# Routing of a PEER layer: picked places compared, multiplied and summed on VectorE, place numbers shifted and masked once per head

## Chip, core and metric

The kernel runs on one core of a Trainium2 chip. The metric is the device time of one execution in microseconds (us). Engines are called as in the profile: PE (TensorE), DVE (VectorE), ACT (ScalarE), POOL (GpSimd), SP (SyncE, which issues most DMAs).

## What is computed

Two layers of a decoder trunk over 512 tokens of width 1024. Each layer: a modulated norm and one wide projection; an S5 state-space branch; a causal differential attention; gates, an output projection and a residual; then a PEER stage over 128 x 128 single-neuron experts. The change lies in PEER's routing, per token and for 8 heads:

```python
v1, i1 = lax.top_k(s1, 16)            # s1, s2: scores against 128 keys each
v2, i2 = lax.top_k(s2, 16)
cand = (v1[..., :, None] + v2[..., None, :]).reshape(..., 256)
sc, ci = lax.top_k(cand, 16)
e1 = jnp.take_along_axis(i1, ci // 16, axis=-1)
e2 = jnp.take_along_axis(i2, ci % 16, axis=-1)
expert = e1 * 128 + e2
g = jax.nn.softmax(sc, axis=-1)
```

The picked experts' rows of two tables are then used with weights from g and a GELU.

## The kernel before

Tokens lie in four tiles of 128. Tiles 1 to 3 are served densely: all 128 chunks of 128 experts are scored by TensorE, and per token weights, zero for experts that were not picked, are built from the routing by `gates`. Tile 0 is served sparsely: its picked rows are gathered.

`front` holds everything of a layer up to the gates. At its end two streams are interleaved: `routed((1, 2, 3))`, which is `route` for three tiles and then `gates`, and `tail`, which already scores 36 of the 128 chunks (`experts`, `products`: a chunk's table is loaded, cast on ACT (L130), its rest subtracted (L132, here on POOL), and 24 matmuls of three lines, L135 to L137, follow on PE). The program's order is only a wish: a scheduler decides each engine's own order when the kernel is built, and each engine then works through its list in that order and waits where it must.

`route(tiles, ...)` runs m = len(tiles) steps per head, 24 in all for tiles 1 to 3, and 8 for tile 0, whose `route` runs in `sparse` beside the dense stage. A step (hp, j) has

- `ask`: query projection of the next head on PE (L833), copied to SBUF by ACT (pqT, L835);
- `halves`: two score matmuls (L840), then `top16` twice on DVE straight from PSUM (MAX8, MATCH_REPLACE8, FIND_INDEX8), the 16 places cast to floats on ACT (i16f, L846), and the 256 candidate sums on POOL (cand, L848);
- `pairs`, one step later: `top16` over the candidates, place numbers ci; ci >> 4 and ci & 15 on DVE (ij, L857 and L858), cast on ACT (ijf, L860);
- `picked`, two steps later: DVE compares ijf with the numbers 0 to 15 (oh, L866: two halves x 16 places x 16 numbers = 512 elements per partition), POOL multiplies by i16f (L868);
- three steps later DVE sums the products into e12 (L886).

For tiles 1 to 3 the numbers 0 to 15 are read from `at`, a copy in PSUM; for tile 0 from `iota128` in SBUF. After the last step the softmax over csv is made (L894 to L900), and `gates` begins for tile 1: transpositions of e12 and csv on PE (L912, L913), eg on ACT, then 16 times a comparison on DVE (L920), products on POOL (L922) and ACT (L925), and outer products on PE (L938).

`layer_consts` (L141) loads small constants of a layer; lt (L153) holds the four lambda vectors, in a tile of its own in pool sm. `sgt()` (L124) hands out one of three buffers sg of 128 x 512, which the S5 tables, the expert products and others use in turn. Pool sm has three buffers per name where nothing else is said, pool rt one.

Of the kernel before, what the change touches and what calls it, by code (L numbers as in the profile page):

```python
# [11 lines left out]
F32 = mybir.dt.float32  # L12
# [3 lines left out]
U32 = mybir.dt.uint32  # L16
AF = mybir.ActivationFunctionType
ALU = mybir.AluOpType
AX = mybir.AxisListType
# [8 lines left out]
TOPK = 16  # L28
# [32 lines left out]
def trunk(ctx, tc, x, c, ada_w, ada_b, n1, n2, w_in, log_dt, a_re, a_im, b_re, b_im, c_re, c_im, dsk,  # L61
          glu_w, qn, kn, lam, subln, up_w, w_out, wq, pk, u_tab, v_tab, u_t, out):
    nc = tc.nc
    V, S, G, T = nc.vector, nc.scalar, nc.gpsimd, nc.tensor
# [10 lines left out]
    sm = ctx.enter_context(tc.tile_pool(name="sm", bufs=3))  # L75
# [48 lines left out]
    def sgt():  # L124
        return sgp.tile([128, 512], F32, name="sg")
# [15 lines left out]
    def layer_consts(l):  # L141
        dc = keep.tile([128, 4], F32, name=f"dc{l}")
        nc.sync.dma_start(dc, dsk[l])
        dcols.append(dc)
        col = keep.tile([128, 3], F32, name=f"col{l}")
        nc.sync.dma_start(col[:, 0:1], qn[l])
        nc.sync.dma_start(col[:, 1:2], kn[l])
        nc.sync.dma_start(col[:, 2:3], subln[l])
        linit = 0.8 - 0.6 * math.exp(-0.3 * l)
        V.tensor_scalar(col[:, 0:1], col[:, 0:1], 0.125, None, op0=ALU.mult)  # L150
        V.tensor_scalar(col[:, 2:3], col[:, 2:3], 1.0 - linit, None, op0=ALU.mult)
        cols.append(col)
        lt = sm.tile([128, 4, 64], F32, name="lt", bufs=1)  # L153
        nc.sync.dma_start(lt, lam[l:l + 1].to_broadcast([128, 4, 64]))
        V.tensor_tensor(lt[:, 0:2], lt[:, 0:2], lt[:, 2:4], op=ALU.mult)
        l2 = sm.tile([128, 2], F32, name="l2")
        V.reduce_sum(l2, lt[:, 0:2], axis=AX.X)
        S.activation(l2, l2, AF.Exp)
        nl = keep.tile([128, 1], F32, name=f"nlam{l}")
        V.tensor_tensor(nl, l2[:, 1:2], l2[:, 0:1], op=ALU.subtract)  # L160
        V.tensor_scalar(nl, nl, linit, None, op0=ALU.subtract)
        lams.append(nl)
        k2 = keep.tile([128, 2, 128], F32, name=f"pk{l}")
        nc.sync.dma_start(k2, pk[l])
        pks.append(k2)
# [286 lines left out]
    def tok(i):  # L452
        return slice(128 * i, 128 * i + 128)
# [32 lines left out]
    def front(l, xsrc, mcol, raw, last, big, rstack, fp, mmp, bup, trp, atp, spec, tail):  # L486
# [326 lines left out]
        def top16(src, n, vals, ids):  # L813
            tmp = rt.tile([128, 256], F32, name="tmp")
            V.max(vals[:, 0:8], src)
            V.match_replace(tmp[:, :n], vals[:, 0:8], src, NEG)  # L816
            V.max(vals[:, 8:16], tmp[:, :n])
            V.max_index(ids[:, 0:8], vals[:, 0:8], src)
            V.max_index(ids[:, 8:16], vals[:, 8:16], tmp[:, :n])

        def route(tiles, pqt, pst, io):

            m, wide = len(tiles), [128, 2, TOPK, TOPK]
            steps = [(hp, j) for hp in range(PH) for j in range(m)]
            query, st = {}, {}

            def ask(hp, s):
                if s == 0:
                    query[hp] = rt.tile([128, 2, ND], F32, name="pqT", bufs=2), load_w(wq[l], 256 * hp, D, nw=256)
                pqT, w = query[hp]  # L830
                pq = pqt()[:, :128 * m]
                for k in range(8):
                    T.matmul(pq.rearrange("p (t n) -> p t n", n=128), w[k][:, 128 * s:128 * s + 128], hts[tiles][:, :, k],  # L833
                             start=(k == 0), stop=(k == 7))
                S.copy(pqT[:, s, :128 * m], pq)  # L835

            def halves(hp, j):
                pss = pst()
                for s in range(2):
                    T.matmul(pss[:, 128 * s:128 * s + 128], query[hp][0][:, s, tok(j)], pks[l][:, s], start=True, stop=True)  # L840
                v16 = sm.tile([128, 2, TOPK], F32, name="v16")
                i16 = sm.tile([128, 2, TOPK], U32, name="i16")
                for s in range(2):
                    top16(pss[:, 128 * s:128 * s + 128], 128, v16[:, s], i16[:, s])
                i16f = sm.tile([128, 2, TOPK], F32, name="i16f")
                S.copy(i16f, i16)  # L846
                cand = rt.tile([128, TOPK, TOPK], F32, name="cand", bufs=2)
                G.tensor_tensor(cand, v16[:, 0].unsqueeze(2).to_broadcast([128, TOPK, TOPK]),  # L848
                                v16[:, 1].unsqueeze(1).to_broadcast([128, TOPK, TOPK]), op=ALU.add)
                st[hp, j] = i16f, cand  # L850

            def pairs(hp, j):
                i16f, cand = st[hp, j]
                ci = sm.tile([128, TOPK], U32, name="ci")
                top16(cand.rearrange("p a b -> p (a b)"), 256, csv[tiles[j]][:, hp], ci)
                ij = sm.tile([128, 2, TOPK], U32, name="ij")
                V.tensor_single_scalar(ij[:, 0], ci, 4, op=ALU.logical_shift_right)  # L857
                V.tensor_single_scalar(ij[:, 1], ci, 15, op=ALU.bitwise_and)  # L858
                ijf = sm.tile([128, 2, TOPK], F32, name="ijf")
                S.copy(ijf, ij)  # L860
                st[hp, j] = i16f, ijf

            def picked(hp, j):
                i16f, ijf = st[hp, j]
                oh = rt.tile([128, 2, TOPK, TOPK], F32, name="oh", bufs=1)
                V.tensor_tensor(oh, ijf.unsqueeze(3).to_broadcast(wide),  # L866
                                io[:, 0:TOPK].unsqueeze(1).unsqueeze(1).to_broadcast(wide), op=ALU.is_equal)
                G.tensor_tensor(oh, oh, i16f.unsqueeze(2).to_broadcast(wide), op=ALU.mult)  # L868
                st[hp, j] = oh

            for i in tiles:
                e12[i] = rt.tile([128, 2, PH, TOPK], F32, name="e12", bufs=3)
            ask(0, 0)
            ask(0, 1)
            for n in range(len(steps) + 3):
                if n < len(steps):
                    hp, j = steps[n]
                    halves(hp, j)
                    for s in range(2):
                        if hp + 1 < PH and j == max(m - 2 + s, 0):  # L880
                            ask(hp + 1, s)
                if 0 <= n - 1 < len(steps):
                    pairs(*steps[n - 1])
                if n >= 3:
                    hp, j = steps[n - 3]
                    V.reduce_sum(e12[tiles[j]][:, :, hp], st.pop((hp, j)), axis=AX.X)  # L886
                if 0 <= n - 2 < len(steps):
                    picked(*steps[n - 2])
                if n < len(steps):
                    yield 5  # L890
            for i in tiles:
# [54 lines left out]
        mg, hts, e12, xts = {}, {}, {}, {}  # L946
        csv = {i: keep.tile([128, PH, TOPK], F32, name=f"csv{i}" + ("" if i in DENSE else f"_{l}")) for i in range(4)}
# [29 lines left out]
        with phase(f"l{l}", [("lp", 1)], []) as (tp,):  # L977
            rt = rstack.enter_context(tc.tile_pool(name=f"r{l}", bufs=1))
# [323 lines left out]
```

## Time and profile before

| what | us |
|---|---|
| median of 3 runs | 3679.18 (3678.8 to 3679.29) |
| the profiled execution, its own time | 3686.12 |
| its span, first to last instruction | 3684.4 |
| busy: PE, DVE, ACT, POOL | 3503.5, 2635.5, 1386.9, 1304.4 |
| routing of tiles 1 to 3 | 508 to 691 in layer 0, 2330 to 2514 in layer 1 |
| gates | 716 to 873 and 2540 to 2697 |

The span is 1.7 us shorter than the execution's time. Busy times are unions of the records of an engine; matmuls are pipelined and their ends are modelled, so that a busy PE need not be PE at its peak. A wait is the idle time of an engine before an instruction, put down to what ended it.

### The profile page before, as it was taken

How to read it: one execution, taken by the hardware profiler on the slowest of the kernel's cores; microseconds unless marked ns; L12 is line 12 of the kernel's file. 1: busy time of each engine (PE TensorE's matmuls, PEld its weight loads, DVE VectorE, ACT ScalarE, POOL GpSimd, SP SyncE). 2: the span in 40 equal slices, each digit the busy share in tenths (PEclk: the TensorE clock that was granted, in tenths of full speed). 3: DMA queues.
4: the chain of work that ended last, by engine and by line, in shares of the span. 5: the costliest groups of instructions: out<-in, count | busy, mean ns of one | idle time of the engine just before them, and what ended most of it. 6: DMA issues, size and time to landing. Idle time of an engine off the chain costs nothing.

```text
span 3684.4 us, 50752 instructions
## 1 busy us (share of the span) xinstructions
PE 3503.5 (95%) x18546; PEld 2928.1 (79%) x18546; DVE 2635.5 (72%) x5033; ACT 1386.9 (38%) x2403; POOL 1304.4 (35%) x931
## 2 busy tenths in 40 slices
PE   8998999899999999999999989998999999999999
PEld 6764677798888888888888647677988888888888
DVE  5855267867678887788977453687666777778887
ACT  3353232475333333333342532325633333333332
POOL 1101134552025554444411001445511544544442
PEclk8998999999999999999999989999999999999999
DMA  7634243478679998998855242435775888999986
GB/s 236 205 115 152 88 149 101 147 220 274 208 277 315 339 327 317 328 339 315 308 198 170 87 152 86 155 115 165 219 252 169 302 327 318 326 329 334 334 313 221
DMA packets 404358, 859.97 MB, mean 233 GB/s; under 512 B 37470, under 2 KB 206430, under 8 KB 400012
## 3 DMA queue, kind: packets, MB, share of 16 engines
q1 hardware_dynamic: 317488, 578.68, 46.0%
q0 software_dynamic: 74304, 270.57, 20.6%
q10 hardware_dynamic: 12316, 7.47, 0.8%
q8 instruction: 146, 2.39, 0.3%
q14 instruction: 104, 0.85, 0.1%
HBM read 769.94 MB, written 86.68 MB: 233 GB/s over the span
## 4 chain that ended last, share of the span: by engine, by line
PE 65%; DVE 15%; DMA 8%; POOL 4%; ACT 4%; issue 2%; SPq 0%; POOLq 0%; DVEq 0%; ACTq 0%
PE acc L135 8%; PE acc L136 8%; PE acc L137 8%; PE sc L135 7%; PE sc L137 7%; PE sc L136 7%; DMA big<-wd 6%; PE mm L547 4%; PE bu L938 3%; PE mm L137 3%; PE mm L135 2%; PE mm L136 2%; DVE wh L132 2%; POOL oh L868 1%; DVE tmp L816 1%
## 5 line engine op out<-in xcount | busy, mean ns | idle before, releaser
L130 ACT CAST wh<-wt 128x1024 fp32r<-128x1024 f32 x592 | 620.7, 1050 | 1008.9 <-PE sc L135 477.1
L132 DVE TENSOR_TENSOR wh<-wt,wh 128x1024 fp32r<-128x1024 f32 x520 | 635.6, 1226 | 254.0 <-ACT wh L130 247.9
L135 PE MATMUL sc<-hh,wh 128*128 128x384 f32 (+1 forms) x2112 | 730.3, 346 | 11.3 <-DVE wh L132 5.6
L137 PE MATMUL sc<-hh,wh 128*128 128x384 f32 (+1 forms) x2112 | 714.2, 338 | 0.0
L136 PE MATMUL sc<-hl,wh 128*128 128x384 f32 (+1 forms) x2112 | 712.4, 338 | 0.3 <-DVE hl L474 0.3
L135 PE MATMUL acc<-wh,gl 128*128 128x512 f32 x1536 | 618.3, 403 | 41.0 <-DVE gl L1042 40.5
L136 PE MATMUL acc<-wh,gh 128*128 128x512 f32 x1536 | 610.5, 397 | 0.5 <-DVE wh L132 0.5
L137 PE MATMUL acc<-wh,gh 128*128 128x512 f32 x1536 | 610.8, 398 | 0.0
L1095 POOL DMA_INDIRECT gt<-in_u_tab_dram,idx x256 | 402.7, 1573 | 390.9 <-DVE junk L1103 330.5
L1095 POOL DMA_INDIRECT gt<-in_v_tab_dram,idx x256 | 343.3, 1341 | 457.3 <-DVE acc L1107 393.6
L135 PEld LDWEIGHTS sc<-hh,wh 128*128 128x128 f32 x2112 | 404.1, 192 | 25.6 <-DVE wh L132 7.1
L136 PEld LDWEIGHTS sc<-hl,wh 128*128 128x128 f32 x2112 | 403.9, 191 | 12.6 <-DVE hl L474 0.6
L137 PEld LDWEIGHTS sc<-hh,wh 128*128 128x128 f32 x2112 | 403.3, 191 | 0.3
L135 PEld LDWEIGHTS acc<-wh,gl 128*128 128x128 f32 x1536 | 290.6, 189 | 111.7 <-DVE gl L1042 52.2
L137 PEld LDWEIGHTS acc<-wh,gh 128*128 128x128 f32 x1536 | 290.6, 189 | 70.9
L136 PEld LDWEIGHTS acc<-wh,gh 128*128 128x128 f32 x1536 | 291.1, 190 | 60.8 <-ACT wh L130 0.9
L1107 DVE SCALAR_TENSOR_TENSOR acc<-gt,act,acc 128x1024 f32<-128x1024 f32 x254 | 326.8, 1287 | 2.3
L1103 DVE SCALAR_TENSOR_TENSOR junk<-gt,h 128x1024 bf16<-128x1024 f32 x256 | 312.0, 1219 | 2.2 <-DMA gt<-in_u_tab_dram,idx 0.3
L920 DVE TENSOR_TENSOR big<-eg,at 128x2048 f32<-128x2048 f32 x96 | 218.9, 2286 | 101.0 <-PE bu L938 44.9
L938 PE MATMUL bu<-big 128*128 128x128 f32 x1536 | 194.3, 279 | 22.2 <-POOL big L922 17.8
L938 PEld LDWEIGHTS bu<-big 128*128 128x128 f32 x1536 | 183.0, 192 | 36.1 <-POOL big L922 31.8
L132 POOL TENSOR_TENSOR wh<-wt,wh 128x1024 fp32r<-128x1024 f32 x72 | 172.8, 2400 | 54.1 <-ACT wh L130 40.7
(330 smaller groups left out, 4966.5 us busy)
## 6 DMA issues: line engine op xcount, KB each, us to landing
wt<-in_u_t_dram SPq DMA_DIRECT2D x256, 512.0 KB
wt<-in_v_tab_dram SPq DMA_DIRECT2D x256, 512.0 KB
big<-wd SPq DMA_DIRECT2D x32, 1536.0 KB
wt<-in_ada_w_dram SPq DMA_DIRECT2D x72, 512.0 KB
wt<-in_w_in_dram SPq DMA_DIRECT2D x64, 512.0 KB
wt<-in_wq_dram SPq DMA_DIRECT2D x64, 512.0 KB
wd<-big SPq DMA_DIRECT2D x24, 1024.0 KB
wd<-stg SPq DMA_DIRECT2D x24, 1024.0 KB
```

Source lines behind the costliest of these rows:

```text
L130: S.copy(hi, raw)
L132: return hi, lo, eng.tensor_tensor(lo, raw, hi, op=ALU.subtract).ins
L135: T.matmul(p, a[1], b[0], start=first, stop=False)
L136: T.matmul(p, a[0], b[1], start=False, stop=False)
L137: return T.matmul(p, a[0], b[0], start=False, stop=last).ins
L547: T.matmul(p, act[:, k, tok(i)], w[k], start=(k == 0), stop=(k == len(w) - 1))
L816: V.match_replace(tmp[:, :n], vals[:, 0:8], src, NEG)
L920: V.tensor_tensor(slots[:, :, b % 2], eg[:, 0:2, 8 * b:8 * b + 8].unsqueeze(3).to_broadcast([128, 2, 8, 128]), io, op=ALU.is_equal)
L938: T.matmul(p[:, j], ob[:, 4 * q + j], og[:, 4 * q + j], start=True, stop=True)
L1095: G.indirect_dma_start(out=t, out_offset=None, in_=tab, in_offset=bass.IndirectOffsetOnAxis(ap=idx[:, k:k + 1], axis=0))
L1103: V.scalar_tensor_tensor(junk, t, 1.0, h2, op0=ALU.mult, op1=ALU.mult, accum_out=act[:, k:k + 1])
L1107: V.scalar_tensor_tensor(acc, t, act[:, k:k + 1], acc, op0=ALU.mult, op1=ALU.add)
```

## The change

In `route`: the product (L868) goes from POOL to DVE, and the sum follows it at once, in `picked` itself. The places of a head's m tiles are collected in one tile ci; shift, mask and cast to floats are then made once per head, for all m tiles, after the last tile's `pairs`. `picked` therefore runs m + 1 steps behind `halves` where it ran two steps behind; i16f has six buffers in place of three, ijf two, and ci, ij and ijf move from pool sm to pool rt. In `layer_consts` lt is no longer a tile of its own but the first half of an sg buffer.

```diff
-        lt = sm.tile([128, 4, 64], F32, name="lt", bufs=1)
+        lt = sgt()[:, 0:256].rearrange("p (k n) -> p k n", k=4)
...
-                i16f = sm.tile([128, 2, TOPK], F32, name="i16f")
+                i16f = sm.tile([128, 2, TOPK], F32, name="i16f", bufs=6)
...
             def pairs(hp, j):
                 i16f, cand = st[hp, j]
-                ci = sm.tile([128, TOPK], U32, name="ci")
-                top16(cand.rearrange("p a b -> p (a b)"), 256, csv[tiles[j]][:, hp], ci)
-                ij = sm.tile([128, 2, TOPK], U32, name="ij")
-                V.tensor_single_scalar(ij[:, 0], ci, 4, op=ALU.logical_shift_right)
-                V.tensor_single_scalar(ij[:, 1], ci, 15, op=ALU.bitwise_and)
-                ijf = sm.tile([128, 2, TOPK], F32, name="ijf")
-                S.copy(ijf, ij)
-                st[hp, j] = i16f, ijf
+                if j == 0:
+                    st[hp] = rt.tile([128, 3, TOPK], U32, name="ci")[:, 0:m]
+                top16(cand.rearrange("p a b -> p (a b)"), 256, csv[tiles[j]][:, hp], st[hp][:, j])
+                st[hp, j] = i16f
+                if j == m - 1:
+                    ij = rt.tile([128, 3, 2, TOPK], U32, name="ij")[:, 0:m]
+                    V.tensor_single_scalar(ij[:, :, 0], st[hp], 4, op=ALU.logical_shift_right)
+                    V.tensor_single_scalar(ij[:, :, 1], st[hp], 15, op=ALU.bitwise_and)
+                    st[hp] = rt.tile([128, 3, 2, TOPK], F32, name="ijf", bufs=2)[:, 0:m]
+                    S.copy(st[hp], ij)
 
             def picked(hp, j):
-                i16f, ijf = st[hp, j]
+                i16f, ijf = st.pop((hp, j)), st[hp][:, j]
...
-                G.tensor_tensor(oh, oh, i16f.unsqueeze(2).to_broadcast(wide), op=ALU.mult)
-                st[hp, j] = oh
+                V.tensor_tensor(oh, oh, i16f.unsqueeze(2).to_broadcast(wide), op=ALU.mult)
+                V.reduce_sum(e12[tiles[j]][:, :, hp], oh, axis=AX.X)
...
-            for n in range(len(steps) + 3):
+            for n in range(len(steps) + m + 1):
...
-                if n >= 3:
-                    hp, j = steps[n - 3]
-                    V.reduce_sum(e12[tiles[j]][:, :, hp], st.pop((hp, j)), axis=AX.X)
-                if 0 <= n - 2 < len(steps):
-                    picked(*steps[n - 2])
+                if 0 <= n - m - 1 < len(steps):
+                    picked(*steps[n - m - 1])
```

The scheduler's order moves with it. VectorE, before, in the middle of layer 0's routing of tiles 1 to 3: a step's search among the candidates ends (L815 to L819), then come shift, mask, comparison and sum.

```order
L816 MATCH_REPLACE tmp<-csv_147,cand 128x256
L815 MAX csv_148<-cand 128x8
L817 MAX csv_147<-tmp 128x8
L818 MAX_INDEX ci<-csv_148,cand 128x8
L819 MAX_INDEX ci<-csv_147,tmp 128x8
L857 TENSOR_SCALAR ij<-ci 128x16
L858 TENSOR_SCALAR ij<-ci 128x16
L866 TENSOR_TENSOR oh<-ijf,at 128x512
L886 TENSOR_REDUCE e_3874<-oh 128x2x16
```

The same place with the change, whose lines 860, 861, 868, 870 and 871 are shift, mask, comparison, product and sum: first the shift and mask of a head, then, nine rows on, its first comparison.

```order
L860 TENSOR_SCALAR ij<-ci 128x3x16
L861 TENSOR_SCALAR ij<-ci 128x3x16
```

```order
L868 TENSOR_TENSOR oh<-ijf,at 128x512
L819 MAX_INDEX i_4746<-v_4745,tmp 128x8
L870 TENSOR_TENSOR oh<-oh,i16f 128x512
L816 MATCH_REPLACE tmp<-csv_146,cand 128x256
L871 TENSOR_REDUCE e_3873<-oh 128x2x16
L817 MAX csv_146<-tmp 128x8
L815 MAX csv_147<-cand 128x8
```

The shift and mask serve three tiles, and comparison, product and sum follow one another on one engine with at most a few searches between them.

GpSimd, before, at the end of the same routing, where the gates' first product (L922) comes up behind the last products of the routing and the early chunks' subtractions (L132):

```order
L132 TENSOR_TENSOR wh<-wt,wh 128x1024
L868 TENSOR_TENSOR oh<-oh,i16f 128x512
L848 TENSOR_TENSOR cand<-v_5510 128x256
L132 TENSOR_TENSOR wh<-wt,wh 128x1024
L868 TENSOR_TENSOR oh<-oh,i16f 128x512 x2
L132 TENSOR_TENSOR wh<-wt,wh 128x1024
L922 TENSOR_TENSOR big<-big,eg 128x640
```

With the change (its L921 is the gates' product):

```order
L132 TENSOR_TENSOR wh<-wt,wh 128x1024
L848 TENSOR_TENSOR cand<-v_5414 128x256
L132 TENSOR_TENSOR wh<-wt,wh 128x1024 x4
L921 TENSOR_TENSOR big<-big,eg 128x640
L132 TENSOR_TENSOR wh<-wt,wh 128x1024
L921 TENSOR_TENSOR big<-big,eg 128x640 x6
```

The products are gone from GpSimd, and four subtractions stand in a row ahead of the gates. On TensorE the list is the same up to the last score matmul of the routing; from there to the first transposition of the gates 38 matmuls of early chunks stood before, and 88 now.

## Rows read from the trace of the kernel before

**Rows 1.** Busy time by stage: us, busy us (records) per engine, granted PE clock, DMA.
```profile
508.00:691.00 183.00, 166.61 (x757) 135.18 (x755) 147.00 (x654) 46.11 (x104) 94.95 (x68) 0.96 0.38 129
...
716.00:873.00 157.00, 148.43 (x1092) 142.30 (x1091) 105.64 (x48) 110.65 (x259) 83.26 (x56) 1.00 0.76 222
2330.00:2514.00 184.00, 166.14 (x763) 134.52 (x763) 147.49 (x656) 46.85 (x104) 94.83 (x68) 0.97 0.39 129
```

**Rows 2.** Waits between 500 and 715 us: total us, times, longest.
```profile
DVE e L886 <- POOL oh L868: 25.4, 22, 1.5
...
PE bu L840 <- ACT pqT L835: 11.5, 6, 3.4
...
DVE oh L866 <- ACT ijf L860: 4.3, 13, 0.3
```

**Rows 3.** Timeline of VectorE, one step: start us, us, then [idle before <- releaser].
```profile
599.39 0.17 DVE L857 TENSOR_SCALAR ij<-ci 128x16 uint32<-128x16 uint32 x1
599.47 0.17 DVE L858 TENSOR_SCALAR ij<-ci 128x16 uint32<-128x16 uint32 x1
599.98 0.69 DVE L866 TENSOR_TENSOR oh<-ijf,at 128x512 f32<-128x512 f32 x1 [0.34 <-ACT ijf L860]
602.12 0.69 DVE L886 TENSOR_REDUCE e<-oh 128x32 f32<-128x512 f32 x1 [1.46 <-POOL oh L868]
```

**Rows 4.** Timeline of GpSimd, the same step.
```profile
600.81 1.28 POOL L868 TENSOR_TENSOR oh<-oh,i16f 128x512 f32<-128x512 f32 x1 [3.12 <-DVE oh L866]
```

**Rows 5.** Timeline of TensorE at full granted clock, two places.
```profile
557.47 5.33 PE L833 MATMUL mm<-h,wt 128*128 128x384 f32 x16
...
594.01 0.33 PE L135 MATMUL sc<-hh,wh 128*128 128x384 f32 x1
...
594.53 0.33 PE L135 MATMUL sc<-hh,wh 128*128 128x384 f32 x1
```

**Rows 6.** Groups by line, 507 to 691 us: count, busy us, mean ns, idle before.
```profile
L833 PE MATMUL mm<-h,wt 128*128 128x384 f32 x224 | 74.6, 486 | 0.0
L135 PE MATMUL sc<-hh,wh 128*128 128x384 f32 x147 | 56.6, 385 | 0.0
...
L132 POOL TENSOR_TENSOR wh<-wt,wh 128x1024 fp32r<-128x1024 f32 x21 | 50.7, 2416 | 17.2 <-ACT wh L130 17.2
...
L840 PE MATMUL bu<-pk,pqT 128*128 128x128 f32 x94 | 16.6, 288 | 11.5 <-ACT pqT L835 11.5
...
L857 DVE TENSOR_SCALAR ij<-ci 128x16 uint32<-128x16 uint32 x22 | 9.8, 445 | 0.5
```

**Rows 7.** Shifts of the whole run (min/median/max ns), and a long one beside GpSimd.
```profile
L857 DVE TENSOR_SCALAR ij<-ci x64: 151/175/2107, 521.6 to 2856.5; 128x16 uint32<-128x16 uint32 x64
...
588.98 2.35 POOL L132 TENSOR_TENSOR wh<-wt,wh 128x1024 fp32r<-128x1024 f32 x1 [2.14 <-ACT wh L130]
589.25 2.10 DVE L857 TENSOR_SCALAR ij<-ci 128x16 uint32<-128x16 uint32 x1
```

**Rows 8.** Timeline behind the routing: scaling of csv on VectorE, a product on GpSimd.
```profile
696.74 1.28 POOL L868 TENSOR_TENSOR oh<-oh,i16f 128x512 f32<-128x512 f32 x1 [3.37 <-DVE sg L899]
696.78 1.39 DVE L900 TENSOR_TENSOR csv<-csv,sg 128x128 f32<-128x128 f32 x1
...
698.97 0.28 DVE L900 TENSOR_TENSOR csv<-csv,sg 128x128 f32<-128x128 f32 x1
```

**Rows 9.** The gates' comparisons of the whole run: min/median/max ns.
```profile
L920 DVE TENSOR_TENSOR big<-eg,at x96: 2235/2289/2292, 702.0 to 2689.0; 128x2048 f32<-128x2048 f32 x96
```

**Rows 10.** Busy time in four us behind an idle spell of TensorE; columns as in rows 1.
```profile
600.00:604.00 4.00, 3.62 (x12) 3.63 (x13) 2.51 (x10) 1.66 (x3) 3.19 (x2) 0.50 0.14 51
```

**Rows 11.** A wait of the whole run, and busy time around tile 0's routing.
```profile
DVE e L886 <- POOL oh L868: 67.4, 56, 1.8
...
873.00:1040.00 167.00, 161.69 (x887) 141.58 (x886) 118.99 (x329) 56.07 (x97) 16.86 (x16) 0.99 0.68 237
```

**Rows 12.** The tile lt: its two loads and their first use, ns and first and last start us.
```profile
L154 SPq DMA_DIRECT2D lt<-in_lam_dram x2: 328/398/467, 44.8 to 111.7; - x2
L155 DVE TENSOR_TENSOR lt<-lt x2: 280/281/282, 72.1 to 889.0; 128x128 f32<-128x128 f32 x2
```

## The prediction

> **What bounds the kernel now.** I read the windows by stage first, then who waits for whom inside the stage that the change edits, then the instructions of one step in order of time, then the groups by line.
>
> The change edits the routing, which runs twice per layer: for token tiles 1 to 3 (24 steps, 8 heads by 3 tiles, beside TensorE's early expert products) and for tile 0 (8 steps, beside the dense stage). The windows show the first one as 183 us in layer 0 and 184 us in layer 1 [rows 1]. VectorE is busy for 147.0 of the 183 us, TensorE is modelled busy for 166.6. Yet it is VectorE's order that sets the pace. The waits between 500 and 715 us name it: VectorE's sums wait 25.4 us for GpSimd's products and its comparisons 4.3 us for ScalarE's casts, while TensorE's score matmuls wait 11.5 us for a ScalarE copy that stands in ScalarE's queue behind casts of VectorE's results [rows 2]. One step in order of time shows the shape: the pair of shift and mask (0.25 us from first start to last end), 0.34 us idle for the cast, the comparison of 0.69 us, 1.46 us idle for GpSimd, the sum of 0.69 us [rows 3]. GpSimd's product takes 1.28 us of that [rows 4].
>
> How much faster could the stage be before TensorE stops it? Matmuls of the early products start 0.173 us apart (three in 0.52 us), sixteen of a query projection take about 5.16 us when followed closely (5.33 as shown, with the last one's tail) [rows 5]. Before the first gate transposition TensorE issues 440 of the former (147 of each of three lines, one less of one of them), 224 of the latter in this window, and 94 score matmuls [rows 6]. At full pace that is 440 x 0.173 = 76, 14 x 5.16 = 72, and about 10 for the scores (their busy time of 16.6 us counts overlaps): 158 of 183 us. So there are some 25 us to win per layer, and TensorE's own list is the floor.
>
> The stage behind it, gates, is 157 us with TensorE busy for 148.4 [rows 1]: whatever TensorE has done earlier is off that list.
>
> **The change, part by part (per layer, the 24-step routing).**
>
> A. The wait for GpSimd's product goes: **-25.4** [rows 2].
>
> B. The wait for the cast goes: **-4.3** [rows 2]. The order of the changed kernel has nine other VectorE rows between the shift and mask and the first comparison that needs them. If ScalarE's queue is late with the cast, a wait is back; it can then be met once per head and not three times.
>
> C. Shift and mask, once a head: 16 of 24 pairs go, 16 x 0.25 = -4.0; the eight that stay work on 48 numbers in place of 16, for which no row stands; I take 0.07 us each, +0.5 (bounds 0 and 8 x 0.5, a pair's worth twice over). Beyond that, 22 shifts took 9.8 us where 22 x 0.17 would be 3.7 [rows 6]: 6.1 us of stall. One of them stands by itself: 2.10 us, ending as a GpSimd subtraction ends that began 0.27 us earlier [rows 7]. With 8 shifts in place of 24 I scale it to 2.0: -4.1. Sum **-7.6**.
>
> D. The products on VectorE: 24 x 0.69 = **+16.5**, the duration of the comparison of the same shape [rows 3]. Bounds: 0.69 and GpSimd's own 1.28 [rows 4]; I take 0.69, the same engine's row.
>
> E. The products' own stalls. The comparison reads one operand from SBUF and one from PSUM (at); the moved product reads both, oh and i16f, from SBUF. Rows for such instructions: the product that scales csv took 1.39 us where the next took 0.28, beginning with a GpSimd instruction and ending as it ended [rows 8]; the gates' comparison, with one operand in PSUM, never left 2.24 to 2.29 us beside a busy GpSimd [rows 9]. So each product can stall as the shift did. The shift met 6.1 us in 24 tries; the product has the same exposure, 24 tries against the same 21 to 23 subtractions of about 2.4 us: **+6.1**. Bounds: 0, if the order keeps them apart, and 23 x 2.4 = 55, if each subtraction catches a product whole.
>
> The Trainium skill ("SBUF — State Buffer", section "Who interferes with whom") speaks against moving this very operation: a VectorE instruction with two SBUF inputs and a GpSimd instruction that reads SBUF exclude each other for the whole of the one that starts first. The rows on csv agree. By that rule alone, with subtractions filling 50.7 of 183 us [rows 6] and half of one, 1.2 us, left on average, E would be 24 x 0.28 x 1.2 = 8 in place of 6.1: an estimate, and the gain would be 2 us smaller per layer.
>
> Sum of VectorE's path: -25.4 - 4.3 - 7.6 + 16.5 + 6.1 = **-14.7**.
>
> F. What TensorE makes of it. The order on TensorE is the same up to the last score matmul; but then 88 early-product matmuls stand ahead of the first gate transposition, where 38 stood. 50 more are 50 x 0.173 = 8.7 us, so its list to that point is 158 + 9 = 167 of 183 - 14.7 = 168 us. It must then hardly ever idle, and it idles 16.4 now [rows 1]. Right behind an idle spell (600 to 604 us) the granted clock stood at 0.50, the lower of its two levels, 1.2 GHz [rows 10]: idling is paid again there. I give back **+5**, something under half of the 11.5 us that its scores wait now; bounds 0 and 11.5.
>
> G. Those 50 matmuls are gone from the gates: at most -8.7, at least 0 (if the comparison, GpSimd and the outer products go round at their own pace). TensorE is busy there for 95%, which speaks for the first; but busy is modelled, and matmuls overlap; I take half, **-4.3**.
>
> Per layer -14.7 + 5 - 4.3 = -14, twice: **-28**.
>
> H. Tile 0's routing, beside the dense stage: 8 products add 5.5 us to VectorE per layer; the waits for GpSimd that go are (67.4 - 2 x 25.4) / 2 = 8.3 [rows 2, 11]. TensorE is busy there for 161.7 of 167 us [rows 11] and covers both: **0**, bounds -1 and +2.
>
> I. lt, the lambda vectors, moves from a tile of its own to one of the three sg buffers. Its loads left SyncE at 44.8 and 111.7 us, long before their use at 72.1 and 889.0 [rows 12]; now layer 0's load waits for a free sg buffer, later in SyncE's queue, and the S5 tables' copies, that use the same three buffers, follow it: on TensorE one group of table matmuls stands some 70 small matmuls later. That stretch has other work on TensorE; I take **+1**, bounds -2 and +4. In layer 1 the load stands ahead of the dense stage by more than 10 us: 0. Moving the other small tiles to another pool costs nothing: no instruction hangs on it.
>
> Sum: -27. The profiled execution took 3686.1 us, 6.9 above the median of the runs shown, 3679.2; against its own time that gives 3659, and against the median **3652**.
>
> **The rivals.**
>
> *Stalls eat it (slower).* E at half a subtraction per product, 24 x 1.19 = 28.6, is 22.5 over my value: A to E give +7.8, G gives nothing, twice +7.8 and +1: 3696. It decides from 0.87 us of stall per product ((25.4 + 4.3 + 7.6 - 16.5) / 24). For it: GpSimd, freed of products, starts each subtraction as soon as its cast is there, and in the changed order four stand in a row just ahead of the gates, beside the last products and csv's scaling. Against: the median of 64 shifts, 0.175 us, shows that most met nothing [rows 7]. Chance 0.06.
>
> *TensorE was the bound all along (no change).* Its list of 167 us, its waits for ScalarE's copies and the clock after each idle spell keep F at 11.5, and the gates go round at their own pace (G 0): -14.7 + 11.5 = -3 per layer, 3679 - 6 + 1 = 3674. For it: 166.6 busy of 183. Against: in the same window it idles whenever VectorE is late. Chance 0.11.
>
> *More comes (faster still).* F 0 and G whole: -14.7 - 8.7 = -23.4 per layer, 3679 - 47 + 1 = 3633; without stalls TensorE's floor stops it some 7 us per layer further on. For it: with VectorE no longer waiting, ScalarE's queue moves on and TensorE never leaves full clock. Chance 0.19.
>
> **How the numbers follow.** The forecast has the rest, 0.64, with a range of its own of 3638 to 3666 (F and G at their other halves). The whole range, 3630 to 3672, takes in most of the third rival and leaves out the slower one and the larger part of the second, and a little below: 0.2 in all. A measurement of this kernel tells 0.2%, some 7 us, from no change; 3671.8 and below is faster: the forecast and the last rival, 0.83; same 0.11; slower 0.06.
>
> **What would show it.** In the changed profile: no wait of VectorE for oh on GpSimd; a group of 64 products on VectorE with a median of 0.69 us, and a maximum that tells E (sum over 24 less 24 x 0.69: 6 us expected); 8 shifts in each of the 24-step routings; that stage 8 to 12 us shorter with VectorE busy above 0.88 of it; the gates 3 to 6 us shorter; table loads at 60 to 110 us not over 4 us later. The forecast is wrong if the products' median itself is above 0.9 us, if the scores' wait for ScalarE's copies grows, or if the stage is shorter and the gates longer by as much.

## The result, and the profile after

The changed kernel takes **3636.7 us** in the median of six runs (3629.0 to 3642.0); the kernel before, in six runs, 3679.0 (3674.5 to 3685.9). The ratio is 0.988 (95% interval 0.987 to 0.9895): **faster by 42 us**. Forecast were 3652 and -27 us: the sign and the whole range hold, the measured gain is half as much again as the forecast one.

The two profiled spans, 3684.4 and 3633.9 us, differ by 50.5 us, and single executions of one kernel lie up to some 15 us apart. So I compare by stage, between events that both programs have: from the first score matmul of the routing of tiles 1 to 3 to the first comparison of the gates, from there to the last outer product of the gates, and both together. Here are the windows of before (layer 0: routing, gates, both; then both in layer 1); the columns are us, busy us (records) per engine, granted PE clock, DMA share and GB/s:

```profile
core 0: us, PE busy (x) PEld busy (x) DVE busy (x) ACT busy (x) POOL busy (x), PEclk, DMA share, GB/s
506.25:702.02 195.77, 179.11 (x821) 147.21 (x820) 157.26 (x691) 54.75 (x118) 99.90 (x71) 0.95 0.37 126
702.02:871.90 169.88, 157.71 (x1153) 150.75 (x1152) 116.14 (x54) 119.04 (x276) 94.64 (x62) 1.00 0.73 214
506.25:871.90 365.65, 336.83 (x1972) 297.95 (x1971) 273.40 (x744) 173.79 (x393) 194.54 (x133) 0.97 0.54 167
2329.20:2694.70 365.50, 336.85 (x1972) 297.62 (x1971) 273.69 (x744) 173.74 (x393) 194.72 (x133) 0.98 0.54 167
```

The same windows of the changed kernel, between the same events:

```profile
506.10:687.19 181.09, 176.00 (x849) 145.18 (x848) 164.67 (x683) 53.24 (x104) 76.42 (x50) 0.99 0.43 140
687.19:851.80 164.61, 152.61 (x1125) 145.79 (x1124) 114.61 (x54) 115.45 (x271) 89.14 (x60) 1.00 0.73 216
506.10:851.80 345.70, 328.62 (x1972) 290.97 (x1971) 279.27 (x736) 168.69 (x375) 165.56 (x109) 1.00 0.58 176
2304.30:2649.40 345.10, 329.01 (x1972) 291.09 (x1971) 279.07 (x736) 168.59 (x375) 165.52 (x109) 1.00 0.58 177
```

The routing is 14.7 us shorter, the gates 5.3, together 20.0 in layer 0 and 20.4 in layer 1: 40 of the 42 us. TensorE does the same 1972 records in both, so the 20 us can be read off its account: idle 365.65 - 336.83 = 28.8 us before and 17.1 after, **11.7 less idle**; and 336.83 busy before, 328.62 after, **8.2 less busy** for the same work, at a mean granted clock of 0.97 before and 1.00 after. Some idle spells are paid twice, as [rows 10] let one suspect. Two matmuls of an early chunk, 0.9 us behind the end of a wait of 3.38 us for ScalarE's copy, in the kernel before:

```profile
600.38 0.80 PE L840 MATMUL bu<-pk,pqT 128*128 128x128 f32 x2 [3.38 <-ACT pqT L835]
...
601.29 0.52 PE L136 MATMUL sc<-hl,wh 128*128 128x384 f32 x1
601.61 0.52 PE L137 MATMUL sc<-hh,wh 128*128 128x384 f32 x1
```

They start 0.32 us apart, where [rows 5] has 0.173 at full clock. In the whole stretch the granted clock stood at its lower level, 1.2 GHz, for 20.5 us in layer 0 and 17.1 in layer 1 before, and for 3.4 us in each layer of the changed kernel, whose score matmuls hardly wait for ScalarE's copies any more. Half of 20.5 - 3.4 is 8.5 us, against the 8.2 less busy. In the second profile of before, below, it is 13.7 us with the same busy time, so that by this account 5 to 8.5 of the 8 us are the clock's.

Now VectorE. The waits of the changed kernel from 506 to 687 us (total, times, longest):

```profile
DVE v L815 <- PE bu L840: 14.9, 7, 7.8
DVE csv L815 <- POOL cand L848: 6.0, 3, 3.4
...
PE bu L840 <- ACT pqT L835: 1.2, 1, 1.2
```

Neither wait of [rows 2] on VectorE is left (25.4 for GpSimd's product, 4.3 for the cast). In their place VectorE waits for scores: 14.9 us, where the same view of before has 8.3, of which 7.8 at the start in both; and 6.0 for the candidate sums, before 4.3. The groups by line in the same window (count, busy us, mean ns):

```profile
L870 DVE TENSOR_TENSOR oh<-oh,i16f 128x512 f32<-128x512 f32 x24 | 19.5, 813 | 0.2
...
L860 DVE TENSOR_SCALAR ij<-ci 128x48 uint32<-128x48 uint32 x8 | 1.6, 199 | 0.2
L861 DVE TENSOR_SCALAR ij<-ci 128x48 uint32<-128x48 uint32 x8 | 1.5, 190 | 0.0
```

The eight pairs of shift and mask take some 3 us, where 22 shifts alone took 9.8 [rows 6]. The products take 19.5 us: 21 of them the usual 0.67 to 0.69, and three take 1.50, 1.62 and 2.15. One of the three in order of time, with the subtraction on GpSimd that holds it:

```profile
645.23 2.35 POOL L132 TENSOR_TENSOR wh<-wt,wh 128x1024 fp32r<-128x1024 f32 x1 [1.74 <-ACT wh L130]
...
645.98 2.15 DVE L870 TENSOR_TENSOR oh<-oh,i16f 128x512 f32<-128x512 f32 x1
```

It began 0.75 us behind the subtraction and ended half a us after it (645.23 + 2.35 = 647.58; 648.13). And an undisturbed one shows that 0.68 us of duration are not 0.68 us of VectorE's time:

```profile
535.47 0.68 DVE L870 TENSOR_TENSOR oh<-oh,i16f 128x512 f32<-128x512 f32 x1
536.06 0.09 DVE L816 MATCH_VALUE_LOAD tmp<-csv,cand 128x8 f32 x1
```

The next instruction starts 0.59 us after it: neighbours overlap by 0.09.

lt, last. The S5 tables' copies in layer 0 start 2 to 6 us later and end 2 to 4 us later than before. Before, then after (L278 and L302, count, min/median/max ns, first and last start):

```profile
L302 ACT COPY sg<-bu x12: 250/257/261, 74.2 to 90.0; 32x128 f32<-32x128 f32 x12
...
L278 ACT COPY sg<-bu x8: 582/588/593, 68.5 to 91.6; 128x512 f32<-128x512 f32 x8
```

```profile
L302 ACT COPY sg<-bu x12: 250/257/259, 80.6 to 92.4; 32x128 f32<-32x128 f32 x12
...
L278 ACT COPY sg<-bu x8: 578/587/593, 70.2 to 95.5; 128x512 f32<-128x512 f32 x8
```

The routing begins at 506.1 against 506.3, and at 505.4 against 504.1 in the second profiles of both kernels: what lt cost lies between nothing and 1 us, and the runs do not tell more.

### The profile page after: what moved, and what is told of

It reads as the page before. It is cut to its first block, busy times and chain, and to the rows that moved or that the text cites. A ratio compares the mean times of both kernels' runs of the same rounds, so it can differ in the third digit from the quotient of the medians.

```text
span 3633.9 us, 50579 instructions
## 1 busy us (share of the span) xinstructions
PE 3480.5 (96%) x18546; PEld 2911.7 (80%) x18546; DVE 2655.9 (73%) x5033; ACT 1376.9 (38%) x2367; POOL 1221.2 (34%) x867
## 4 chain that ended last, share of the span: by engine, by line
PE 70%; DVE 11%; DMA 8%; POOL 3%; ACT 3%; issue 2%; DVEq 0%; SPq 0%; ACTq 0%; POOLq 0%
PE acc L135 8%; PE acc L137 8%; PE acc L136 8%; PE sc L135 7%; PE sc L137 7%; PE sc L136 7%; DMA big<-wd 6%; PE mm L547 4%; PE mm L833 3%; PE bu L937 3%; PE mm L137 3%; PE mm L136 3%; PE mm L135 3%; DVE wh L132 2%; PE sc L833 1%
## 5 line engine op out<-in xcount | busy, mean ns | idle before, releaser
L132 DVE TENSOR_TENSOR wh<-wt,wh 128x1024 fp32r<-128x1024 f32 x520 | 634.1, 1223 | 257.1 <-ACT wh L130 252.0
L132 POOL TENSOR_TENSOR wh<-wt,wh 128x1024 fp32r<-128x1024 f32 x72 | 173.4, 2411 | 124.0 <-ACT wh L130 111.8
```

The costliest lines, as they stand in the source:

```text
L132: return hi, lo, eng.tensor_tensor(lo, raw, hi, op=ALU.subtract).ins
```

## The experiments

Two theories stood against each other. The prediction's: VectorE's path sets the routing, and each us on it is a us of the whole. Its rival: in the changed kernel TensorE's own list has become the floor.

### The kernel before, profiled again

> The kernel before, profiled a second time, to see which part of the 50.5 us between the two profiled spans (3684.4 and 3633.9) belongs to the change. In the two traces the routing of tiles 1 to 3 with the gates is 20 us shorter in each layer, and the dense stage behind them 5 us shorter in each. Theory: the dense stage's 5 us are a slower execution of before, not the change; a second profile shows a span near 3677 with the same routing and gates (from 506 to 872 in layer 0) and dense stages 3 to 5 us shorter. Rival: the dense stage gains by the change (tile 0's routing without waits for GpSimd); then this profile repeats the dense stages of the first to within 1 us.

Measured: span 3679.0. Routing and gates in the two layers, then the dense stages behind them:

```profile
504.10:869.60 365.50, 336.25 (x1972) 297.14 (x1971) 273.49 (x744) 173.48 (x394) 194.57 (x133) 0.98 0.55 167
2323.10:2688.40 365.30, 336.27 (x1972) 297.20 (x1971) 273.52 (x744) 173.52 (x394) 194.61 (x133) 0.98 0.55 167
869.60:1888.40 1018.80, 984.80 (x5064) 861.48 (x5062) 816.75 (x1332) 361.96 (x549) 405.30 (x280) 0.99 0.86 304
2688.40:3673.30 984.90, 964.21 (x4800) 850.61 (x4798) 749.81 (x1100) 331.77 (x473) 383.99 (x272) 0.99 0.82 295
```

The changed kernel's dense stages:

```profile
851.80:1869.70 1017.90, 983.01 (x5065) 860.31 (x5063) 819.64 (x1340) 362.02 (x549) 390.52 (x272) 0.99 0.85 304
2649.40:3628.30 978.90, 962.64 (x4800) 849.11 (x4799) 754.26 (x1108) 331.77 (x473) 373.32 (x264) 1.00 0.83 297
```

Routing and gates repeat to 0.2 us, so 20 us per layer is the change's. The dense stage does not repeat: layer 0's took 1023.1 us in the first profile of before and 1018.8 in this one, against 1017.9 after. Its 5 us there are one execution's, as the theory said. In layer 1 it repeats (984.0 and 984.9), as the rival said, and the changed kernel's 978.9 is 5 to 6 us shorter; whether that is the change's stays open, since the kernels below with nearly the same work there spread from 976 to 989 us.

### The product twice

```diff
                 V.tensor_tensor(oh, oh, i16f.unsqueeze(2).to_broadcast(wide), op=ALU.mult)
+                if m > 1:
+                    V.tensor_tensor(oh, oh, i16f.unsqueeze(2).to_broadcast(wide), op=ALU.min)
```

> For tiles 1 to 3 a second instruction of the product's shape and operands stands behind each product (the smaller of product and i16f, which leaves the values as they are): 24 more per layer, some 0.61 us each net of overlap, and 3 us of stalls beside GpSimd. Theory (VectorE's list still sets the pace of the routing, so a microsecond there is a microsecond of the whole): 14.7 + 3 = 18 us per layer, 3637 + 35 = 3672, that is a ratio to before of 0.998. Rival (TensorE is the bound now; VectorE's waits for scores, 16 us per layer in the changed kernel, take the added work up): at most 3 us per layer, 3643, ratio 0.990.

Measured: 3657.5 us, ratio 0.993 (0.992 to 0.995): 21 us slower than the changed kernel, halfway between the two theories. Routing and gates of layer 0, and a wait and the added group in the routing:

```profile
508.50:863.00 354.50, 331.69 (x1972) 292.48 (x1971) 296.45 (x760) 168.21 (x375) 167.75 (x109) 0.99 0.56 172
```

```profile
DVE v L815 <- PE bu L840: 8.0, 2, 7.8
```

```profile
L872 DVE TENSOR_TENSOR oh<-oh,i16f 128x512 f32<-128x512 f32 x24 | 21.7, 902 | 0.1
```

VectorE is busy 17.2 us longer per layer (296.45 - 279.27), the stage 8.8. The wait for scores fell from 14.9 to 8.0: VectorE had 7 us of slack there, and most of what is added beyond it counts.

### The product left out

```diff
-                V.tensor_tensor(oh, oh, i16f.unsqueeze(2).to_broadcast(wide), op=ALU.mult)
+                if m == 1:
+                    V.tensor_tensor(oh, oh, i16f.unsqueeze(2).to_broadcast(wide), op=ALU.mult)
```

> For tiles 1 to 3 the product is left out (tile 0 keeps it), so that the sums are counts of hits and the gates' weights go to other experts; nothing else is changed. VectorE's list loses 17.9 us net per layer. Theory (VectorE sets the pace): 3637 - 36 = 3601, ratio 0.979. Rival (TensorE is the bound now): TensorE is idle for only 5.1 us between the first score matmul and the first gate comparison, so at most that is to be had per layer: 3627, ratio 0.986.

Measured: 3639.4 us, ratio 0.990 (0.988 to 0.991). **Nothing is gained**; that is even less than the rival allowed. Routing alone, then routing and gates, and the wait for scores:

```profile
504.15:679.30 175.15, 170.60 (x821) 140.07 (x820) 148.15 (x659) 52.54 (x102) 72.94 (x49) 1.00 0.43 144
504.15:851.10 346.95, 330.43 (x1972) 293.08 (x1971) 262.80 (x712) 169.92 (x375) 164.68 (x109) 0.99 0.57 176
```

```profile
DVE v L815 <- PE bu L840: 24.8, 8, 7.8
```

VectorE's list is 16.5 us shorter (279.27 to 262.80). Of that, 9.9 turned into waiting for scores. The routing's end came 6 us sooner (175.2 for 181.1), but with 28 fewer records of TensorE done by then (821 for 849); they were done in the gates, and the two together take 347 us in layer 0 and 349 in layer 1, no less than with the product (345.7 and 345.1). So a shorter list on VectorE than the changed kernel's wins nothing: TensorE was idle for 5.1 of the routing's 181.1 us with the product, and for 4.6 of 175.2 without it.

### Shift, mask and cast per step again

```diff
-                if j == m - 1:
-                    ij = rt.tile([128, 3, 2, TOPK], U32, name="ij")[:, 0:m]
...
+                ij = sm.tile([128, 2, TOPK], U32, name="ij")
+                V.tensor_single_scalar(ij[:, 0], ci, 4, op=ALU.logical_shift_right)
+                V.tensor_single_scalar(ij[:, 1], ci, 15, op=ALU.bitwise_and)
+                ijf = sm.tile([128, 2, TOPK], F32, name="ijf")
+                S.copy(ijf, ij)
...
-                if 0 <= n - m - 1 < len(steps):
-                    picked(*steps[n - m - 1])
+                if 0 <= n - 2 < len(steps):
+                    picked(*steps[n - 2])
```

> The product stays on VectorE with the sum right behind it, but shift, mask and cast are made per step again, as in the kernel before, two steps behind. Theory (shift and mask once a head is a part of the gain, by VectorE's path): 16 pairs with their stalls come back, +9.2 us per layer, and the wait for ScalarE's cast, +4.5: 3637 + 27 = 3664, ratio 0.996. Rival (nearly all of the gain is the wait for GpSimd, the rest is taken up by VectorE's waits for scores): +3 per layer at most, 3643, ratio 0.990.

Measured: 3658.8 us, ratio 0.995 (0.994 to 0.9965), 22 us slower than the changed kernel. Layer 0, and two waits in its routing:

```profile
503.66:861.80 358.14, 333.10 (x1972) 295.27 (x1971) 292.43 (x768) 174.15 (x393) 168.44 (x109) 0.99 0.56 170
```

```profile
PE bu L840 <- ACT pqT L835: 7.5, 5, 2.3
DVE oh L866 <- ACT ijf L860: 4.8, 14, 0.4
```

The cast's wait is back (4.8), VectorE is busy 13.2 us longer, and TensorE's scores again wait for ScalarE's copies, 7.5 us for 1.2, since the casts per step stand among them in ScalarE's queue again (read from its order; not tried alone). Moving the product alone thus brings 7.5 to 10 us per layer (365.6 to 358.1 in layer 0, 355.1 in layer 1), not 20.

### Shift, mask and cast per head alone, the product on GpSimd

```diff
-                V.tensor_tensor(oh, oh, i16f.unsqueeze(2).to_broadcast(wide), op=ALU.mult)
-                V.reduce_sum(e12[tiles[j]][:, :, hp], oh, axis=AX.X)
+                G.tensor_tensor(oh, oh, i16f.unsqueeze(2).to_broadcast(wide), op=ALU.mult)
+                st[hp, j] = oh
...
+                if n >= m + 2:
+                    hp, j = steps[n - m - 2]
+                    V.reduce_sum(e12[tiles[j]][:, :, hp], st.pop((hp, j)), axis=AX.X)
```

> Shift, mask and cast once a head as in the changed kernel, but the product back on GpSimd and its sum one step later, ahead of the next comparison. VectorE's list loses the product (17.9 us net per layer) and gets the waits for GpSimd back (25.4 before). Leaving the product out altogether gave nothing (3639 against 3637), so VectorE's list is no longer what counts below some 165 us. Theory (TensorE's own list is the floor of the changed kernel, and 147 net + 25 of waits = 172 us of VectorE's path still fit under it): 3637 to 3642, ratio 0.989 to 0.990, that is, the product's move brought nothing that the other half does not bring alone. Rival (the waits for GpSimd are on the path of the routing whatever TensorE does): + 7.5 us per layer, 3652, ratio 0.993; or the whole gain of the move, 8.5 us per layer as between before and the run with mask per step: 3654, ratio 0.993.

Measured: 3645.2 us, ratio 0.991 (0.989 to 0.992):

```profile
505.70:854.00 348.30, 331.22 (x1972) 293.53 (x1971) 265.39 (x712) 171.10 (x377) 194.65 (x133) 0.99 0.57 175
```

```profile
DVE e L888 <- POOL oh L870: 14.6, 12, 2.9
DVE v L815 <- PE bu L840: 13.3, 6, 7.8
```

348 us per layer: **this half alone brings 17.3 of the 20 us.** VectorE waits for GpSimd here, and yet also for scores (13.3 us): it is not late enough to matter. The time lies between my theory's 3642 and the rival's 3652; by the profile 2.6 us per layer are left to the product's move, by the medians 8 us in all, with intervals that overlap a little. The halves do not add up: 17 alone and 7.5 to 10 alone make 20, which fits a second bound near 345 us. This half also lets the comparison run m + 1 steps behind in place of two, and VectorE's waits for GpSimd fall from 25.4 to 14.6 us with the product still there. Whether the later comparison or the fewer small instructions brought the more was not tried: no run has shift and mask per step with the comparison m + 1 steps behind.

### i16f read from PSUM

```diff
-                i16f = sm.tile([128, 2, TOPK], F32, name="i16f", bufs=6)
+                if m > 1:
+                    k = 128 + 32 * (steps.index((hp, j)) % 6)
+                    i16f = iof[:, k:k + 32].rearrange("p (s t) -> p s t", s=2)
+                else:
+                    i16f = sm.tile([128, 2, TOPK], F32, name="i16f", bufs=6)
```

> For tiles 1 to 3 the operand i16f of the product is written to PSUM (a free part of the bank of the numbers 0 to 15), so that the product reads one operand from SBUF and one from PSUM; nothing else is changed. Theory on the stall (only an instruction with all its inputs in SBUF is held by a GpSimd subtraction): no product of the three tiles above 0.75 us, where three of 24 took 1.50 to 2.15 us. Rival: the same products stay long. On the time: with TensorE as the floor 3637 within 3, ratio 0.988; with VectorE's path as the bound 2 x 3.2 us less, 3630, ratio 0.987.

Measured: 3638.0 us, ratio 0.989 (0.987 to 0.991). The products of tiles 1 to 3 of both layers, and one beside a subtraction:

```profile
L874 DVE TENSOR_TENSOR oh<-oh,at x48: 662/670/689, 537.2 to 2482.5; 128x512 f32<-128x512 f32 x48
```

```profile
582.37 2.37 POOL L132 TENSOR_TENSOR wh<-wt,wh 128x1024 fp32r<-128x1024 f32 x1 [0.97 <-ACT wh L130]
583.12 0.67 DVE L874 TENSOR_TENSOR oh<-oh,at 128x512 f32<-128x512 f32 x1
```

It starts 0.75 us behind the subtraction, just as the product that took 2.15 us did, and takes 0.67. Of the 48, 16 began inside a subtraction, and none is above 0.69. So the operand's place is what made the stall, as the rule named in the prediction (the Trainium skill, "SBUF — State Buffer", "Who interferes with whom") has it. On the time this run decides nothing. The products are 3.4 us shorter in layer 0, but others got longer, the softmax's subtractions over csv by 2.3 us, and VectorE's list of the stretch is only 0.7 us shorter (278.58 for 279.27); ScalarE is busy 6 us longer, and the stretch takes 348.8 and 345.8 us.

### Late subtractions on VectorE

```diff
-                        keys.append(experts(l, EARLY[n + 1]))
+                        keys.append(experts(l, EARLY[n + 1], G if n < 22 else V))
```

> The last 13 of the 36 early chunks' subtractions per layer, which fall into the gates, go from GpSimd to VectorE. In the gates of the changed kernel TensorE is idle for 12 us per layer, in most cases waiting for GpSimd's product, which stands behind a subtraction of 2.4 us. Theory (these idle spells are what is left to win on TensorE's floor): half of them go, 6 us per layer, 3637 - 12 = 3625, ratio 0.985. Rival (the 13 x 1.2 = 16 us on VectorE delay the gates' comparisons, which fill 110 of VectorE's 165 us there): 3637 or above.

Measured: 3634.6 us, ratio 0.987 (0.986 to 0.989), not told apart from the changed kernel's. In layer 0 the stretch takes 346.3 us, its gates 166.6 with TensorE idle for 10.1:

```profile
503.30:849.60 346.30, 330.93 (x1972) 292.28 (x1971) 294.65 (x749) 168.68 (x376) 143.19 (x96) 0.99 0.58 176
683.00:849.60 166.60, 156.54 (x1139) 148.72 (x1138) 131.54 (x67) 116.77 (x274) 70.36 (x48) 1.00 0.73 214
```

The theory misses: the subtractions stand behind at most 2 of TensorE's 12 idle us in the gates. The rival's time holds within the noise, its reason does not: 17 us more on VectorE there cost nothing that the runs can tell. No version here beats the changed kernel by more than the measurement can tell.

### The product in bf16

```diff
-                i16f = sm.tile([128, 2, TOPK], F32, name="i16f", bufs=6)
+                i16f = sm.tile([128, 2, TOPK], BF16, name="i16f", bufs=6)
...
-                oh = rt.tile([128, 2, TOPK, TOPK], F32, name="oh", bufs=1)
+                oh = rt.tile([128, 2, TOPK, TOPK], BF16, name="oh", bufs=1)
```

> The comparison's result and i16f are made in bf16 in place of f32 (the place numbers up to 127 are exact in it), the sum stays f32. What the product then takes is not known: bounds 0.3 and 0.67 us. Theory (TensorE's list is the floor): the time stays at 3637 within 4 whatever the product takes, ratio 0.988. Rival (VectorE's path is the bound): every 0.1 us on a product is 2.4 us per layer, 3637 - 14 = 3623 if the product falls to 0.37.

Measured: 3639.6 us, ratio 0.988 (0.9865 to 0.990). The products' min/median/max in the whole run, then the 24 of layer 0's routing as a group:

```profile
L870 DVE TENSOR_TENSOR oh<-oh,i16f x64: 400/424/2465, 535.6 to 2815.9; 128x512 bf16<-128x512 bf16 x64
```

```profile
L870 DVE TENSOR_TENSOR oh<-oh,i16f 128x512 bf16<-128x512 bf16 x24 | 18.2, 759 | 0.2
```

The median product falls to 0.42 us and the time does not move. This does not decide between the theories either: six of the 24 were now caught by a subtraction (1.25 to 2.45 us), three in f32, so that the group takes 18.2 us for 19.5 and VectorE's list is only 1.6 us shorter (277.64 for 279.27). The rival's 14 us for the whole rested on a gain that did not come.

### 32 early chunks, and the changed kernel again

```diff
-NPRE = 36
+NPRE = 32
```

> The changed kernel with 32 early chunks per layer in place of 36: 96 matmuls of 0.173 us, 16.6 us, leave TensorE's list between the first score matmul of the routing and the end of the gates, and come back in the dense stage. The stretch took 345.7 us in layer 0 with 36 chunks (329 busy and 17 idle). Theory (TensorE's list is the floor of that stretch): it becomes some 16 us shorter, 329 to 332, and the dense stage some 16 longer, so that the whole stays at 3637 within 6, ratio 0.987 to 0.990. Rival (VectorE's path and the gates' round trip set the stretch): it stays at 345 with TensorE idle for 33 us, and the whole is 2 x 16.6 longer, 3670, ratio 0.998.

> The changed kernel as it is, once more, beside the run with 32 early chunks and with a second profile, since the runs are to be compared to within some us: 3637 within 3, ratio 0.988, and from the first score matmul to the end of the gates 345 to 346 us in each layer.

Measured: the changed kernel 3632.5 us (ratio 0.987, 0.985 to 0.989; 345.0 and 346.2 us per layer), with 32 chunks 3644.1 (0.990, 0.988 to 0.992), 1 us above the theory's 3637 + 6 and far from the rival's 3670. Layer 0 with 32 chunks, both stages and the gates:

```profile
503.90:840.20 336.30, 315.40 (x1876) 276.18 (x1875) 279.07 (x736) 163.76 (x367) 157.94 (x105) 0.99 0.57 173
680.40:840.20 159.80, 144.59 (x1069) 136.11 (x1068) 114.84 (x55) 112.63 (x267) 84.18 (x57) 1.00 0.71 209
```

With 96 matmuls (16.6 us) fewer the stretch is 9.4 us shorter in layer 0 and 7.2 in layer 1 (337.9 for 345.1), half of what a pure TensorE floor would give. The routing is 4.6 us shorter (176.5 for 181.1). The gates are 4.8 us shorter and TensorE is idle in them for 15.2 us where it was 12.0. In the routing TensorE is idle for 5.7 us, about as little as with 36 chunks (5.1), and follows its list; in the gates a shorter list turns in part into idle time behind the round trip of comparison, product and outer product. So TensorE's list bounds the stretch in part, and the other engines' path lies close behind it: neither is the only bound.

## Why the prediction was right, and where its size was off

- **What bounds the kernel.** Right: VectorE's order did set the routing's pace, and 20 us per layer came out of it. Also right that TensorE's list lies close behind: F put 167 us against a path of 168, and in the changed kernel leaving the product out won nothing more.
- **A and B**, the waits for GpSimd (-25.4) and the cast (-4.3): both gone, as predicted.
- **C**, shift and mask: forecast -7.6. The two instructions kept VectorE busy for 12.0 us before and 2.5 after, -9.5: none of the eight was caught by a subtraction, where I had left 2.0.
- **D**, 24 products: forecast 16.5 by their duration. They cost some 24 x 0.60 = 14.4, as neighbours overlap by 0.09 us.
- **E**, their stalls: forecast 6.1, measured 3.2 (three of 24 caught: 1.50 + 1.62 + 2.15 - 3 x 0.68). The mechanism is shown by the run with i16f in PSUM. A caught product lost 1.1 us on average, near the 1.2 of half a subtraction; the number caught was off, three where the prediction's second estimate has 24 x 0.28 = 6.7. It moves with small shifts in time (six in bf16), and scaling the shift's stalls could not tell it.
- **F**, what TensorE makes of it: forecast +5, as what would remain of TensorE's own waits for ScalarE's copies. These fell from 11.5 to 1.2 us; in their place VectorE waits, its waits for scores and candidates growing by 6.6 + 1.7 = 8.3. So the step failed in its kind and not only in its size.
- A to F: forecast -9.7, measured -14.7 at the first gate comparison. **C, D and E were sized too dear by 2, 2 and 3 us, F too cheap by 3**; the remaining 1 us was not traced. That A to E alone came to the same -14.7 in the forecast is chance: with the measured values they make -21.6. VectorE is busy for 0.91 of the routing, where above 0.88 was forecast.
- **Where the missing 6 us lie in time.** The forecast's window of the routing, 183 us, and F's list end at the first transposition of the gates (L912, now L911); its window of the gates begins 25 us later. Before, then after:

```profile
691.25 0.69 PE L912 MATMUL tr<-ident,e 128*128 128x128 f32 x2 [5.14 <-DVE e L886]
...
702.02 2.24 DVE L920 TENSOR_TENSOR big<-eg,at 128x2048 f32<-128x2048 f32 x1
```

```profile
680.98 0.69 PE L911 MATMUL tr<-ident,e 128*128 128x128 f32 x2 [3.83 <-DVE e L871]
...
687.19 2.23 DVE L919 TENSOR_TENSOR big<-eg,at 128x2048 f32<-128x2048 f32 x1
```

From the first score matmul to that transposition it took 185.0 us and takes 174.9, 10.1 less, inside the 8 to 12 that the prediction named for the stage. The other 4.6 of the 14.7 us, and of the 6 that the forecast missed, lie between the transposition and the first comparison, 10.8 us before and 6.2 after in both layers, where the prediction had no window. In the kernel before VectorE still searches among the last candidates there (691.4 to 695.7) and waits 1.2 us for GpSimd's last product; with the change every search is over at 677.3. In both kernels TensorE waits for VectorE's sum ahead of the transposition, so that VectorE's path still sets that moment.

- **G**, the gates: forecast -4.3, measured -5.3.
- **H**, tile 0's routing: 0 forecast. From the last outer product to the end of its search it took 161.8 us before and 161.1 after. **I**, lt: +1 forecast, 0 to 1 measured. The sign that the prediction gave for it, table loads not over 4 us later, is missed: the first of the tables' copies L302 starts 6.4 us later.
- Per layer -14 was forecast and -20 measured; 3636.7 lies just outside the forecast's own range (3638 to 3666) and nearer to the third rival's 3633. That rival's reason, that ScalarE's queue moves on and TensorE keeps its full clock, held: 11.5 to 1.2 us of waits, 0.95 to 0.99 of the clock in the routing. Its sum was met in part by luck: its -14.7 for the routing came out of other terms, with F at 8.3 and not 0, and G came to -5.3, not -8.7. The 7 us that it leaves to TensorE's floor do not follow from the prediction's figures, by which 183 - 167 + 8.7 = 24.7 us is the most, 1.3 beyond its 23.4.
- The rival of a TensorE bound all along was wrong for the kernel before (TensorE's idle time fell by 11.7 us) and comes near to being right for the kernel after: without the product nothing more came, while 17 us more on VectorE cost 9.
- The slower rival, stalls of 0.87 us per product, met 3.2 / 24 = 0.13.

## What to carry to other kernels

Cost a moved instruction by the distance to the start of the next one, not by its duration. Read the sum against the list of the engine that stands behind the one that you relieve: here the halves of the change brought 7.5 to 10 and 17 us per layer by themselves, and both together 20, and below that a shorter list on the first engine won nothing. Before moving an operation, try the cheap edit beside it: collecting three small shifts, masks and casts into one, with the comparison two steps later, brought most of this gain, though which of the two did more was not tried. And before an unmoved time is read as a bound, look whether the edit made the list shorter at all: the product in bf16 and the operand in PSUM took only 1.6 and 0.7 us off VectorE's list.

## What the runs showed of the chip

TensorE's busy time for the same 1972 records goes roughly with the time that its granted clock stood at the lower level, 1.2 GHz, rather than with its idle time: 336.8 us busy with 20.5 us at that level and 336.3 with 13.7 (the two profiles of before, 28.8 and 29.3 idle), 333.1 with 10.2 (mask per step, 25.0 idle), 331.2 with 10.2 (mask per head alone, 17.1 idle), 328.6 with 3.4 (the changed kernel, 17.1 idle), and 327.7 with none (i16f in PSUM, layer 1, 18.1 idle).

A product on VectorE with both operands in SBUF can be held by a GpSimd subtraction that began before it: in layer 0's routing four products of the changed kernel began inside one; three took 1.50 to 2.15 us, the fourth, 0.05 us behind the subtraction's start, 0.68. With one operand in PSUM none of 16 was held (at most 0.69). The same product in bf16 takes 0.42 us, but is still held, up to 2.47.
